# Row transposes between the first adaLN chunks, modulation by feature block, and convolution and adaLN halves between the steps of attention

## The chip, the cores and the metric

The kernel runs on one core of a Trainium2 chip. The metric is the time of one execution on the device in microseconds (us), the median of several runs; smaller is better. An engine is named as the profile names it: PE is TensorE, DVE is VectorE, ACT is ScalarE, POOL is GpSimd, and SP is the engine that issues most of the loads.

## The reference, cut to what matters

Two transformer blocks follow each other over 512 tokens of width 1024. The change touches only the mixer of the first one:

```python
mod   = silu(c) @ w_ada + b_ada              # six rows of 1024: shift, scale, gate, twice
mod_c = silu(c_ctx) @ w_ada + b_ada
hc = modulate(rmsnorm(ctx, g_mix), csh1, csc1)        # 256 context tokens
k_c, v_c = split(hc @ w_in[:, 512:768])
h = modulate(rmsnorm(x, g_mix), sh1, sc1)             # h * (1 + scale) + shift
q, k, v, bg, cg, hv = split(h @ w_in)
att  = windowed_attention(rope(q), rope(k), v, k_c, v_c, sink)
u    = cg * hv
conv = bg * (cw[0] * prev(u) + cw[1] * u + cw[2] * next(u))
x = x + gt1 * (concat([att, conv]) @ w_out)
```

After it come a router with 16 experts of 64 tokens each, then the second block: four feed-forward layers of width 2816, a pooling mixer, a latent attention, and a last norm. All products are made in fp32 from high and low halves, so one product is three matmuls (`mm3`).

## The kernel before

**Weights.** The class `Weights` holds one list of chunks in the order of use. `chunk` plans a load of up to 1 MB, issued on SP into a ring of four buffers (`NR`); `unit` plans a part of a chunk. `next()` hands out the next unit. A unit that is not raw is split first into `whi` (ACT, L161) and `wlo` (DVE, L162), in four buffers, two units ahead. A chunk's buffer comes free when its last unit is split, or, for raw units (the adaLN weights `w_ada`), when the next unit is asked for.

**Order on the engines.** The code is written in one order, and a scheduler puts each engine's instructions into a fixed queue; an engine executes its queue in order. Tiles are given out in rotation: `psA`, `psB` and `psC` have two buffers each in the accumulator memory (PSUM), `pA` of 1024 columns and `pB` and `pC` of 512. Who asks for a third waits until the first is read out.

**Stages before attention.** `ada_rows(0)` multiplies eight 1 MB chunks of `w_ada` (L478) while the six tiles of 128 token rows arrive (`xrow`), get their norm (L275, L262) and are scaled (L495). From its result come `sc1` and `sh1` (scale and shift). Then, for each of the six tiles, `turned` transposes the rows on PE (L294) into `pB` or `pC`, and `modulated_into` makes from each of the eight feature blocks the high half on ACT (L519) and the low half on DVE (L522, L523); 24 matmuls make keys and values of the tile. After the six tiles, q is made for all four tiles of `x` in the two buffers of `pA`. `rope1` rotates keys and q on DVE (L540 to L542); q is split (L599, L600), transposed on PE (L605) and stored as `qT` (L606). The convolution has four blocks of channels; each has three units (`cg`, `hv`, `bg`) of 24 matmuls of 512 columns, in turns in `pB` and `pC`, and a chain on DVE (L621 to L626) that ends in `conv`, which lies in the first half of the tile `X`. In the queue of PE, all four blocks stand ahead of the first score.

**Attention.** There are eight steps, one for each pair of token tile and key head. `scores` makes four heads, each in a `pA` (L687, L689, masks L692), takes the maximum on DVE (L694), the exponential on ACT (L696) and scales (L703). `values` transposes each of four or five key blocks on PE into `pB` (L712), splits (ACT L255, DVE L256) and multiplies into a `pC`. The adaLN groups 1 and 2 (`ada_group`, 8 MB of weights each) stand whole before steps 2 and 5.

**After attention.** `w_out` is applied with the convolution's half of the rows first (`project_out`); L786 reads the first finished tile. Then come norm, router and top-k, the experts and the second block. They aren't changed.

Of the kernel before, what the change touches and what calls it, by code (L numbers as in the profile page):

```python
# [9 lines left out]
F32 = mybir.dt.float32  # L10
# [85 lines left out]
def f(ap):  # L96
    return ap.bitcast(F32)
# [93 lines left out]
def tile_net(ctx, tc, I, out):  # L191
# [20 lines left out]
    def psB():  # L212
        return psh[0].tile([P, 512], F32, name="pB", tag="pB")
# [124 lines left out]
    plan_ada(0)  # L338
    plan_cols(w_in, K, 512, 256, 8, 4)
    plan_cols(w_in, K, 0, 512, 4, 2)  # L340
    for c2 in range(2):
        cs = [W.chunk([(0, P, rows(w_in, 0, K, b0 + c2 * 256, 256))], (P, K, 256)) for b0 in (1280, 1792, 768)]
        for cc in range(2):
            for c in cs:
                W.unit(c, lambda v, cc=cc: v[:, :, cc * P:(cc + 1) * P])
    plan_ada(1)
    plan_ada(2)
    for k0 in (4, 6, 0, 2):
        if k0 >= 4:
# [106 lines left out]
    st = ExitStack()  # L456
    early = st.enter_context(tc.tile_pool(name="early", reuse_waits=RW, bufs=1))

    def token_rows(src, t):
        r = early.tile([P, D], F32, name="xrow", tag="xrow", bufs=6)  # L460
# [6 lines left out]
    def ada_rows(pool, g):  # L467


        bb = pool.tile([P, 512], F32, name="bb", tag="rp1", bufs=1)  # L470
# [3 lines left out]
        p = psB()  # L474
        for k in range(K):
            w = W.next()
            for j in range(4):
                PE.matmul(p[32 * j:32 * j + 32], cb[:, k].rearrange("p s c -> p (s c)"), w[:, j],  # L478
                          start=k == 0, stop=k == K - 1)
        V.tensor_add(bb, p, bb)  # L480
        return bb

    def spread(dst, rows_, j):

# [9 lines left out]
    for r in rows_in:  # L494
# [18 lines left out]
    def modulated_into(pool, dst, t, sc, sh, pick=None):  # L513

        def put(g, m, pv):
            for a in range(m):
                k = g + a
                c_ = slice(t * P, (t + 1) * P)
                A.activation(dst[0][:, k, c_], pv[:, a], AF.Identity, scale=sc[:, k:k + 1], bias=sh[:, k:k + 1])  # L519
            tmp = pool.tile([P, 4, P], F32, name="mtmp", tag="mtmp", bufs=1)  # L520
            for a in range(m):
                V.tensor_scalar(tmp[:, a], pv[:, a], sc[:, g + a:g + a + 1], sh[:, g + a:g + a + 1], op0=OP.mult, op1=OP.add)  # L522
            V.tensor_sub(dst[1][:, g:g + m, c_], tmp, f(dst[0][:, g:g + m, c_]))  # L523
        return put

    hcT = qT.rearrange("p h s -> p (h s)").rearrange("p (s k n) -> p s k n", s=2, k=K)
    hcT = [hcT[:, 0], hcT[:, 1]]
    hT = pair("hT")

    def rope1(src, nt, n, t, pool):  # L530

# [14 lines left out]
    ws = [W.next(), W.next()]  # L546
    kvs = Xf[:, 0:6 * 256].rearrange("p (b n) -> p b n", n=256)

    def turned(b):
        xs, t, s = (hcT, b, 1) if b < TC else (hT, b - TC, 0)  # L550
        transposed(rows_in[b], K, modulated_into(early, xs, t, sc1[:, s], sh1[:, s]))
        return xs, t

    nxt = turned(0)
    for b in range(6):
        xs, t = nxt
        if b < 5:
            nxt = turned(b + 1)
        o = psA()[:, 0:256]
        for k in range(K):  # L560
            mm3(o, [x[:, k, t * P:(t + 1) * P] for x in xs], [x[:, k % 4] for x in ws[k // 4]], k == 0, k == K - 1)
        A.copy(out=kvs[:, b], in_=o)
    split(Vh, Vl, kvs[:, :, P:256])
    for b0 in (0, 2, 4):
        kr = kvs[:, b0:b0 + 2, 0:P]
        if b0:
            kr = rope1(kr.rearrange("p b (h d) -> p b h d", d=HD), 2, KV, b0 - 2, early)
        kr = kr.rearrange("p b (g d) -> p b g d", d=HD)
        kpk = early.tile([P, 2, 2, KV, 2, HD], F32R, name="kpk", tag="kpk", bufs=1)
        for s in range(2):  # L570
            for b in range(2):
                A.copy(out=kpk[:, 0, b, :, s], in_=kr[:, b])
        for s in range(2):
            for b in range(2):
                V.tensor_sub(kpk[:, 1, b, :, s], kr[:, b], f(kpk[:, 0, b, :, s]))
        for s in range(2):
            p = psBC()
# [8 lines left out]
    a0, a1 = psA(), psA()  # L586
    qp = [a0[:, 0:512], a0[:, 512:1024], a1[:, 0:512], a1[:, 512:1024]]
    for u in range(4):
        w = W.next()
        for kk in range(2):  # L590
            k = u * 2 + kk
            for t in range(T):
                mm3(qp[t], [x[:, k, t * P:(t + 1) * P] for x in hT], [x[:, kk] for x in w], k == 0, k == K - 1)
    qks = []
    for t in range(T):
        qr = rope1(qp[t].rearrange("p (o h d) -> p o h d", o=1, d=HD), 1, H, t, early)
        qr = qr[:, 0].rearrange("p (h d) -> p h d", d=HD)
        qk = early.tile([P, H, 2, HD], F32R, name="qk", tag="qk", bufs=1)
        A.copy(out=qk[:, :, 0], in_=qr)  # L599
        V.tensor_sub(qk[:, :, 1], qr, f(qk[:, :, 0]))  # L600
        for g in range(2):
            p = psA()
            pv = p[:, :512].rearrange("p (h t) -> p h t", h=4)
# [5 lines left out]
    for cblk in range(4):  # L609
        p3 = []  # L610
        for _ in range(3):
            p3.append(psBC())
            w = W.next()
            for k in range(K):
                mm3(p3[-1], [x[:, k] for x in w], [x[:, k] for x in hT], k == 0, k == K - 1)
        cg = early.tile([P, S], F32, name="cg", tag="rp1", bufs=1)
        A.copy(out=cg, in_=p3[0])
        u_ = early.tile([P, S + 2], F32, name="convu", tag="convu", bufs=1)
        V.memset(u_[:, 0:1], 0.0)
        V.memset(u_[:, S + 1:S + 2], 0.0)  # L620
        V.tensor_mul(u_[:, 1:S + 1], p3[1], cg)  # L621
        y = early.tile([P, S], F32, name="convy", tag="rp2", bufs=1)
        V.tensor_scalar(y, u_[:, 0:S], cw[:, cblk, 0:1], None, op0=OP.mult)
        V.scalar_tensor_tensor(y, u_[:, 1:S + 1], cw[:, cblk, 1:2], y, op0=OP.mult, op1=OP.add)
        V.scalar_tensor_tensor(y, u_[:, 2:S + 2], cw[:, cblk, 2:3], y, op0=OP.mult, op1=OP.add)
        V.tensor_mul(conv[:, cblk], p3[2], y)  # L626
# [5 lines left out]
    mixT = pair("mixT")  # L632
    for cblk in range(4):
        split(mixT[0][:, 4 + cblk], mixT[1][:, 4 + cblk], conv[:, cblk])
# [7 lines left out]
    cl = []  # L642

    def ada_group(g):
        m = ada_rows(att, g)
        p = psB()
        for c in range(2):
            for j in range(2):
# [57 lines left out]
    def values(n, g, Pt, lo, hi):  # L706
# [11 lines left out]
        split(mixT[0][r, 0:4, n * P:(n + 1) * P], mixT[1][r, 0:4, n * P:(n + 1) * P], ov)  # L718

    todo = [(n, g) for n in range(T) for g in range(KV)]  # L720
    nxt = scores(*todo[0])
    for z, (n, g) in enumerate(todo):
# [740 lines left out]
```

## Time and profile before

| | us |
|---|---|
| median of 3 runs (2702.54 to 2704.97) | 2703.97 |
| profiled execution | 2703.63 |
| its span, from first to last instruction | 2701.6 |

The profiled execution is 2.0 us longer than its span and 0.3 us below the median. PE is busy for 95% of the span; the remaining idle time of PE lies almost all in the first 400 us. In the lines of the timeline, the words in brackets say how long an engine was idle before an instruction, and what it waited for. A granted clock of 1.00 is 2.4 GHz on PE, and 0.50 is 1.2 GHz.

### The profile page before, as it was taken

Reading aid. Unit: us, or ns where it says so; the run is one execution under the profiler, and the core shown is the slowest. Engines: PE = TensorE matmul, PEld = TensorE weight load, DVE = VectorE, ACT = ScalarE, POOL = GpSimd, SP = SyncE. Lnnn points to the kernel's source line nnn. Section 1 sums busy time; section 2 is a strip of 40 time slices with the busy share of each in tenths; the row PEclk is TensorE's granted clock in tenths of the full one; section 3 lists DMA queues with packets and bytes.
Section 4 is the critical chain, followed back from the end, with each engine's and each line's share of the span. In section 5 each row is a group of like instructions: output and inputs, shape, how many; then the busy total and the mean of one; then the engine's idle time right before and its main releaser. Section 6 shows DMA issues by size and latency. Waiting matters only on the chain.

```text
span 2701.6 us, 29081 instructions
## 1 busy us (share of the span) xinstructions
PE 2568.8 (95%) x12042; PEld 1879.9 (70%) x12042; DVE 1066.7 (39%) x1661; ACT 748.4 (28%) x1288; POOL 88.5 (3%) x142
## 2 busy tenths in 40 slices
PE   5988979999998999999999999999999899999999
PEld 3864744333433888878877878887879777878887
DVE  4646441222223433335533334333334566533332
ACT  4324320000002322223322223322223655322221
POOL 1000020000000000000000000000001100000000
PEclk8989979999999999999999999999999999999999
DMA  8226249999998322323222322323232111122321
GB/s 301 67 86 221 71 164 419 414 418 418 416 417 342 124 94 90 105 86 102 74 94 90 106 86 86 108 80 102 78 101 73 63 57 63 63 94 78 108 83 59
DMA packets 179251, 411.89 MB, mean 152 GB/s; under 512 B 7364, under 2 KB 120544, under 8 KB 151472
## 3 DMA queue, kind: packets, MB, share of 16 engines
q1 hardware_dynamic: 176928, 403.73, 40.7%
q0 software_dynamic: 1184, 2.97, 0.4%
q10 hardware_dynamic: 1008, 3.34, 0.3%
q8 instruction: 94, 1.54, 0.2%
q14 instruction: 37, 0.30, 0.0%
HBM read 407.92 MB, written 2.10 MB: 152 GB/s over the span
## 4 chain that ended last, share of the span: by engine, by line
PE 58%; issue 30%; DVE 4%; ACT 3%; DMA 3%; POOL 1%; ACTq 0%; POOLq 0%; DVEq 0%; SPq 0%
PE pA L905 8%; PE pA L247 7%; PE pA L248 7%; PE pA L249 7%; PE pB L905 4%; PE pC L248 2%; PE pC L247 2%; PE pC L249 2%; PE pB L249 2%; PE pB L247 2%; PE pB L248 2%; DMA wraw<-in_w_ada_dram 1%; PE pC L879 1%; PE pC L952 1%; PE ms L1334 1%
## 5 line engine op out<-in xcount | busy, mean ns | idle before, releaser
L161 ACT CAST whi<-wraw 128x1024 fp32r<-128x1024 f32 (+2 forms) x334 | 336.2, 1011 | 1107.6 <-PE pA L248 686.3
L162 DVE TENSOR_TENSOR wlo<-wraw,whi 128x1024 fp32r<-128x1024 f32 (+2 forms) x334 | 392.4, 1177 | 480.1 <-ACT whi L161 472.7
L248 PE MATMUL pA<-xTl,whi 128*128 128x512 f32 (+1 forms) x1536 | 578.7, 377 | 1.6 <-DVE xTl L256 1.6
L249 PE MATMUL pA<-xTh,wlo 128*128 128x512 f32 (+1 forms) x1536 | 578.5, 377 | 0.0
L247 PE MATMUL pA<-xTh,whi 128*128 128x512 f32 (+1 forms) x1536 | 574.7, 382 | 1.5 <-ACT xTh L255 1.3
L247 PEld LDWEIGHTS pA<-xTh,whi 128*128 128x128 f32 x1536 | 290.4, 189 | 76.8 <-ACT sl L989 21.6
L249 PEld LDWEIGHTS pA<-xTh,wlo 128*128 128x128 f32 x1536 | 290.4, 189 | 56.6
L248 PEld LDWEIGHTS pA<-xTl,whi 128*128 128x128 f32 x1536 | 290.8, 189 | 55.2 <-DVE xTl L256 2.1
L991 DVE TENSOR_TENSOR sl<-pA,sl 128x512 f32<-128x512 f32 x88 | 60.9, 692 | 427.3 <-PE pA L249 427.2
L905 PE MATMUL pA<-wraw,wideh 128*64 128x512 f32 x736 | 202.6, 598 | 1.9 <-DMA wraw<-in_w_up_dram 1.4
L249 PE MATMUL pC<-whi,hl 128*128 128x512 f32 x352 | 138.4, 393 | 0.0
L247 PE MATMUL pC<-whi,hh 128*128 128x512 f32 x352 | 138.4, 393 | 0.0
L248 PE MATMUL pC<-wlo,hh 128*128 128x512 f32 x352 | 138.4, 393 | 0.0
L247 PE MATMUL pB<-whi,hh 128*128 128x512 f32 x352 | 138.3, 393 | 0.0
L248 PE MATMUL pB<-wlo,hh 128*128 128x512 f32 x352 | 138.2, 392 | 0.0
L249 PE MATMUL pB<-whi,hl 128*128 128x512 f32 x352 | 138.0, 392 | 0.0
L905 PEld LDWEIGHTS pA<-wraw,wideh 128*64 128x64 f32 x736 | 58.3, 136 | 93.2 <-issue 88.2
L905 PE MATMUL pB<-wraw,hx 128*64 128x512 f32 x344 | 101.0, 597 | 1.1 <-DMA wraw<-in_w_down_dram 1.1
L247 PEld LDWEIGHTS pB<-whi,hh 128*128 128x128 f32 x352 | 66.1, 188 | 15.5 <-DVE X L1040 0.8
L249 PEld LDWEIGHTS pB<-whi,hl 128*128 128x128 f32 x352 | 66.1, 188 | 15.1
L247 PEld LDWEIGHTS pC<-whi,hh 128*128 128x128 f32 x352 | 66.1, 188 | 15.0
L248 PEld LDWEIGHTS pB<-wlo,hh 128*128 128x128 f32 x352 | 66.1, 188 | 14.8
(489 smaller groups left out, 3370.4 us busy)
## 6 DMA issues: line engine op xcount, KB each, us to landing
wraw<-in_w_gate_dram SPq DMA_DIRECT2D x47, 1024.0 KB, 13.3
wraw<-in_w_up_dram SPq DMA_DIRECT2D x45, 1024.0 KB, 12.2
wraw<-in_w_down_dram SPq DMA_DIRECT2D x43, 1024.0 KB, 9.3
wraw<-in_ffn_w_gate_dram SPq DMA_DIRECT2D x40, 1024.0 KB, 5.2
wraw<-in_ffn_w_up_dram SPq DMA_DIRECT2D x40, 1024.0 KB, 5.3
wraw<-in_ffn_w_down_dram SPq DMA_DIRECT2D x32, 1024.0 KB, 4.9
wraw<-in_w_ada_dram SPq DMA_DIRECT2D x24, 1024.0 KB, 9.4
widel<-in_w_up_dram SPq DMA_DIRECT2D x14, 1024.0 KB, 14.0
```

Source lines behind the costliest of these rows:

```text
L161: self.nc.scalar.copy(out=hi, in_=src)
L162: self.nc.vector.tensor_sub(lo, src, f(hi))
L247: PE.matmul(o, a[0], b[0], start=first, stop=False)
L248: PE.matmul(o, a[0], b[1], start=False, stop=False)
L249: PE.matmul(o, a[1], b[0], start=False, stop=last)
L879: PE.matmul(p, ohr[:, t], h[:, t, c_], start=t + z == 0, stop=t + z == T)
L905: PE.matmul(outs[dh][r], x[:, k, r], ws[e][:, j, dh * 512:(dh + 1) * 512], start=k == 0, stop=k == K - 1)
L952: PE.matmul(p, Se[:, t * P:(t + 1) * P], ys[dh][s], start=s == 0, stop=s == 1)
L991: V.tensor_mul(sl, a[:, 512:1024], sl)
L1334: PE.matmul(p[:, :nn], q[a][:, c_], k[b][:, :nn], start=first, stop=False)
```

## The change

The token rows lie in one tile, `xrows`. They are transposed and written back in place during the first adaLN group (`between`, after each chunk), before scale and shift are known. `modulated` then works on one feature block of all context tiles or of all `x` tiles. Keys and values of all six tiles are accumulated at once, in one `pA`, both `pB` and both `pC`. The weights of the convolution come in 12 chunks of 0.5 MB. `conv_block` is a generator that gives up control after each unit and uses only `pC`. Block 0 is started after q and runs beside the rotations. Blocks 1 to 3 and the adaLN groups, in halves of four chunks with a sum of their own, are taken after the steps of attention, by the list in `steps`. Attention's output is kept in `attn` (the second half of `X`) and split per token tile (`settle`), since `mixT` takes the memory of `hT`, which the convolution now reads longer.

```diff
+    def plan_conv(u0, u1):
+        for u in range(u0, u1):
+            b0 = (1280, 1792, 768)[u % 3] + u // 3 * P
+            c = W.chunk([(0, P, rows(w_in, 0, K, b0, P))], (P, K, P))
+            W.unit(c, lambda v: v)
+
+    plan_conv(0, 6)
     plan_ada(1)
+    plan_conv(6, 12)
     plan_ada(2)
...
+        for k0 in (0, 4):
+            p = psB() if g else psA()[:, 0:512]
+            for k in range(k0, k0 + 4):
+                w = W.next()
+                for j in range(4):
+                    PE.matmul(p[32 * j:32 * j + 32], cb[:, k].rearrange("p s c -> p (s c)"), w[:, j],
+                              start=k == k0, stop=k == k0 + 3)
+                if between is not None:
+                    between(k)
+            V.tensor_add(bb, p, bb)
+            yield bb
...
+    def turned(b):
+
+        r = rows_in[b]
         V.tensor_scalar(r, r, row_rstd(early, r, D), None, op0=OP.mult)
-    m = ada_rows(early, 0)
+
+        def put(g, m, pv):
+            (A.copy if g else V.tensor_copy)(out=r[:, g * P:(g + m) * P].rearrange("p (a n) -> p a n", n=P), in_=pv)
+
+        transposed(r, K, put)
+
+    *_, m = ada_rows(early, 0, between=lambda k: turned(k) if k < TC + T else None)
...
+    def modulated(xs, s, k):
+
+        x = xrows[:, :TC] if s else xrows[:, TC:]
+        x, sc, sh = x[:, :, k * P:(k + 1) * P], sc1[:, s, k:k + 1], sh1[:, s, k:k + 1]
+        hi, lo = (v[:, k].rearrange("p (b n) -> p b n", n=P) for v in xs)
+        A.activation(hi, x, AF.Identity, scale=sc, bias=sh)
+        V.tensor_scalar(x, x, sc, sh, op0=OP.mult, op1=OP.add)
+        V.tensor_sub(lo, x, f(hi))
...
+    a0 = psA()
+    kvp = [a0[:, 0:256], a0[:, 512:768], psB()[:, 0:256], psB()[:, 0:256], psC()[:, 0:256], psC()[:, 0:256]]
+    for k in range(K):
+        modulated(hcT, 1, k)
+        modulated(hT, 0, k)
+        for b, o in enumerate(kvp):
+            xs, t = (hcT, b) if b < TC else (hT, b - TC)
             mm3(o, [x[:, k, t * P:(t + 1) * P] for x in xs], [x[:, k % 4] for x in ws[k // 4]], k == 0, k == K - 1)
...
+    first = conv_block(early, 0)
+    next(first)
     split(Vh, Vl, kvs[:, :, P:256])
...
     for t in range(T):
+        if t % 2 == 0:
+            next(first)
         qr = rope1(qp[t].rearrange("p (o h d) -> p o h d", o=1, d=HD), 1, H, t, early)
...
+    def steps():
...
+        ada1, ada2 = ada_group(1), ada_group(2)
+        c1, c2, c3 = (conv_block(att, c) for c in (1, 2, 3))
+        some(c1, 3)
+        yield
+        some(ada1, 1)
+        yield
+        some(ada1, 1)
+        some(c2, 1)
+        yield
+        some(c2, 2)
+        yield
+        some(c3, 2)
+        yield
+        some(c3, 2)
+        some(ada2, 1)
+        yield
+        some(ada2, 1)
+        yield
...
     for z, (n, g) in enumerate(todo):
         cur = nxt
-        if z in (1, 4):
-            ada_group(1 if z == 1 else 2)
         if z + 1 < len(todo):
             nxt = scores(*todo[z + 1])
         values(n, g, *cur)
+        next(beside, None)
+        if z == 6:
+            mixT = pair("mixT")
+            for cblk in range(4):
+                split(mixT[0][:, 4 + cblk], mixT[1][:, 4 + cblk], conv[:, cblk])
+            for b in range(T - 1):
+                settle(b)
+    settle(T - 1)
```

Three places show how the queues change. The first is the queue of DVE at the rotation of q's first tile (`rp` is the rotated tile, `pA` holds q, `wlo` the low half of a weight unit, `qk` q split). Before:

```order
L540 TENSOR_TENSOR rp_821<-pA,cst 128x8x32
L541 TENSOR_TENSOR rp_822<-pA,cst 128x8x32
L540 TENSOR_TENSOR rp_821<-pA,cst 128x8x32
L541 TENSOR_TENSOR rp_822<-pA,cst 128x8x32
L542 TENSOR_TENSOR rp_821<-rp_821,rp_822 128x512
L162 TENSOR_TENSOR wlo<-wraw,whi 128x1024
L600 TENSOR_TENSOR qk<-rp_821,qk 128x8x64
```

Now, at the same place:

```order
L552 TENSOR_TENSOR rp_833<-pA,cst 128x8x32
L553 TENSOR_TENSOR rp_834<-pA,cst 128x8x32
L626 CAST kTl<-pB 128x2x256
L552 TENSOR_TENSOR rp_833<-pA,cst 128x8x32
L553 TENSOR_TENSOR rp_834<-pA,cst 128x8x32
L596 TENSOR_TENSOR convu<-pC,cg 128x512
L554 TENSOR_TENSOR rp_833<-rp_833,rp_834 128x512
L598 TENSOR_SCALAR convy<-convu,cw 128x512
L162 TENSOR_TENSOR wlo<-wraw,whi 128x1024
L599 SCALAR_TENSOR_TENSOR convy<-convu,cw,convy 128x512
L636 TENSOR_TENSOR qk<-rp_833,qk 128x8x64
L600 SCALAR_TENSOR_TENSOR convy<-convu,cw,convy 128x512
```

The product `convu`, which needs the second unit of convolution block 0 from PE, now stands between the products of the rotation and their sum.

The second place is the queue of PE where the first scores stand (`pA<-kTh,qT`). Before, the last matmuls of convolution block 3 stand ahead of them, and nothing between the first heads:

```order
L248 MATMUL pC<-hTl,whi 128x512
L249 MATMUL pC<-hTh,wlo 128x512
L687 MATMUL pA<-kTh,qT 128x256
L687 MATMUL pA<-kTl,qT 128x256
L689 MATMUL pA<-kTh,qT 128x256
L689 MATMUL pA<-kTl,qT 128x256
```

Now the last matmuls of block 0 stand ahead, and 24 of the 32 transposes of q (L640) between the first heads:

```order
L248 MATMUL pC<-hTl,whi 128x512
L249 MATMUL pC<-hTh,wlo 128x512
L704 MATMUL pA<-kTh,qT 128x256
L704 MATMUL pA<-kTl,qT 128x256
L706 MATMUL pA<-kTh,qT 128x256
L706 MATMUL pA<-kTl,qT 128x256
L709 LDWEIGHTS identb
L709 MATMUL pA<-nextb,identb 128x128
L640 MATMUL pB<-cst,qk 128x128 x16
```

The 216 matmuls of the blocks 1 to 3 have moved behind: 72 of them after the eighth head, 58 of these in a row, and 144 from the second half of adaLN group 1 to the first half of group 2.

The third place is an adaLN group in the queue of PE. Before, at the end of group 2:

```order
L689 MATMUL pA<-kTl,qT 128x256
L692 LDWEIGHTS identb
L692 MATMUL pA<-prevb,identb 128x128
L478 MATMUL pB<-wraw,cb 32x512 x12
L649 MATMUL pB<-cst,bb 128x128 x4
L486 MATMUL pB<-bb,cst 128x512 x2
```

Now, at the end of group 1's second half:

```order
L484 MATMUL pB<-wraw,cb 32x512 x4
L248 MATMUL pC<-PTl,Vh 128x512
L249 MATMUL pC<-PTh,Vl 128x512
L484 MATMUL pB<-wraw,cb 32x512 x11
L704 MATMUL pA<-kTh,qT 128x256
L704 MATMUL pA<-kTl,qT 128x256
L706 MATMUL pA<-kTh,qT 128x384
L706 MATMUL pA<-kTl,qT 128x384
```

Each half has 16 of these matmuls close together, and a step's scores and values stand between the halves.

## Rows read from the trace of the kernel before

**Rows 1.** The page: span, and 40 equal slices of it, in tenths.

```profile
span 2701.6 us, 29081 instructions
...
PE   5988979999998999999999999999999899999999
...
DMA  8226249999998322323222322323232111122321
```

**Rows 2.** Busy time of each engine in stretches; granted clock, DMA share, GB/s.

```profile
10.00:41.00 31.00, 14.31 (x69) 2.27 (x69) 5.24 (x10) 6.90 (x12) 5.55 (x13) 0.96 1.02 394
45.50:75.20 29.70, 23.27 (x162) 21.40 (x161) 26.93 (x65) 21.87 (x60) 0.00 (x0) 0.88 0.39 127
75.20:101.80 26.60, 26.59 (x134) 22.36 (x135) 15.65 (x36) 8.91 (x17) 2.01 (x4) 1.00 0.16 50
...
122.40:172.84 50.44, 50.44 (x219) 40.65 (x218) 19.07 (x31) 7.95 (x10) 0.00 (x0) 1.00 0.18 65
...
178.70:192.30 13.60, 11.13 (x45) 9.67 (x46) 8.38 (x22) 6.41 (x18) 0.00 (x0) 0.50 0.09 32
...
260.50:267.40 6.90, 6.11 (x20) 2.78 (x12) 3.49 (x6) 3.01 (x4) 0.00 (x0) 0.51 1.06 293
...
291.00:332.10 41.10, 40.80 (x187) 32.87 (x188) 13.33 (x23) 9.49 (x17) 0.00 (x0) 1.00 0.15 52
...
410.00:600.00 190.00, 186.93 (x803) 76.25 (x799) 42.27 (x81) 13.36 (x23) 0.00 (x0) 1.00 1.01 417
```

**Rows 3.** Groups by line, 0 to 420 us: count, then busy us and mean ns.

```profile
L162 DVE TENSOR_TENSOR wlo<-wraw,whi 128x1024 fp32r<-128x1024 f32 x26 | 31.5, 1222 | 33.6 <-ACT whi L161 33.5
...
L522 DVE TENSOR_SCALAR mtmp<-pB,sc,sh 128x128 f32<-128x128 f32 x24 | 8.3, 404 | 0.7 <-DVE qT L523 0.5
...
L523 DVE TENSOR_TENSOR hTl<-mtmp,hTh 128x512 fp32r<-128x512 f32 x8 | 5.5, 688 | 0.1
...
L495 DVE TENSOR_SCALAR xrow<-xrow,rstd 128x1024 f32<-128x1024 f32 x6 | 4.5, 753 | 14.6 <-POOL rstd L263 14.4
```

**Rows 4.** Timeline of DVE at the rotation of q: start us, us, instruction.

```profile
100.66 0.42 DVE L540 TENSOR_TENSOR rp<-pA,cst 128x256 f32<-128x256 f32 x1 [1.82 <-PE pA L249]
...
105.03 0.42 DVE L540 TENSOR_TENSOR rp<-pA,cst 128x256 f32<-128x256 f32 x1
...
110.85 0.42 DVE L540 TENSOR_TENSOR rp<-pA,cst 128x256 f32<-128x256 f32 x1
...
115.30 0.42 DVE L540 TENSOR_TENSOR rp<-pA,cst 128x256 f32<-128x256 f32 x1
...
121.80 0.68 DVE L606 CAST qT<-pA 128x512 fp32r<-128x512 f32 x1
```

**Rows 5.** Timeline where attention starts.

```profile
177.42 1.28 ACT L696 ACT_TABLE_LOAD   x1 [2.37 <-DVE sm L695]
178.72 0.69 ACT L696 ACTIVATE Pt<-pA,sm 128x512 f32<-128x512 f32 x1
...
179.55 0.58 PE L687 MATMUL pA<-kTh,qT 128*128 128x256 f32 x1 [5.59 <-ACT Pt L696]
```

**Rows 6.** What PE waited for, 178.7 to 332.1 us: total us, times, longest.

```profile
PE pA L687 <- ACT Pt L696: 10.9, 10, 5.6
PE pB L478 <- DMA wraw<-in_w_ada_dram: 5.0, 4, 2.7
PE pB L649 <- DVE bb L480: 2.7, 2, 1.9
PE pC L248 <- DVE PTl L256: 2.5, 6, 0.8
```

**Rows 7.** Loads: issuing queue, count, KB each, median us from issue to landing.

```profile
wraw<-in_ffn_w_gate_dram SPq DMA_DIRECT2D x8, 512.0 KB, 3.8
...
X<-in_x_dram POOLq DMA_DIRECT2D x4, 512.0 KB, 8.4
```

More of the change, by code (lines that the diff above doesn't have):

```diff
@@ L340, in tile_net @@
     plan_cols(w_in, K, 0, 512, 4, 2)
[L341 to L345, printed above, removed]
+    def plan_conv(u0, u1):
[4 more added lines that the diff above has]
+    plan_conv(0, 6)
     plan_ada(1)
+    plan_conv(6, 12)
     plan_ada(2)
@@ L457, in tile_net @@
     early = st.enter_context(tc.tile_pool(name="early", reuse_waits=RW, bufs=1))
+    xrows = early.tile([P, TC + T, D], F32, name="xrows")
     def token_rows(src, t):
-        r = early.tile([P, D], F32, name="xrow", tag="xrow", bufs=6)
+        r = xrows[:, t if src is ctx_in else TC + t]
         nc.scalar.dma_start(out=r, in_=src[t * P:(t + 1) * P])
@@ L465, in tile_net, with ada_rows @@
     b_ada = I["b_ada"]
-    def ada_rows(pool, g):
-        bb = pool.tile([P, 512], F32, name="bb", tag="rp1", bufs=1)
+    def ada_rows(pool, g, between=None):
+        bb = pool.tile([P, 512], F32, name="bb", tag="bb" if g else "cg", bufs=1)
         for j in range(4):
@@ L473, in ada_rows @@
             nc.gpsimd.dma_start(out=bb[32 * j:32 * j + 32], in_=b_ada[:, c0:c0 + 512].to_broadcast([32, 512]))
[L474 to L481, printed above, removed]
+        for k0 in (0, 4):
[9 more added lines that the diff above has]
+            yield bb
     def spread(dst, rows_, j):
@@ L547, in tile_net @@
     kvs = Xf[:, 0:6 * 256].rearrange("p (b n) -> p b n", n=256)
[L549 to L560, printed above, removed]
-            mm3(o, [x[:, k, t * P:(t + 1) * P] for x in xs], [x[:, k % 4] for x in ws[k // 4]], k == 0, k == K - 1)
-        A.copy(out=kvs[:, b], in_=o)
+    a0 = psA()
@@ new lines, in tile_net @@
+    kvp = [a0[:, 0:256], a0[:, 512:768], psB()[:, 0:256], psB()[:, 0:256], psC()[:, 0:256], psC()[:, 0:256]]
[4 more added lines that the diff above has]
+            xs, t = (hcT, b) if b < TC else (hT, b - TC)
+            mm3(o, [x[:, k, t * P:(t + 1) * P] for x in xs], [x[:, k % 4] for x in ws[k // 4]], k == 0, k == K - 1)
+    for b, o in enumerate(kvp):
+        (V.tensor_copy if b % 2 else A.copy)(out=kvs[:, b], in_=o)
@@ new lines, in tile_net, with conv_block @@
+    a0, a1 = psA(), psA()
+    qp = [a0[:, 0:512], a0[:, 512:1024], a1[:, 0:512], a1[:, 512:1024]]
+    for u in range(4):
+        w = W.next()
+        for kk in range(2):
+            k = u * 2 + kk
+            for t in range(T):
+                mm3(qp[t], [x[:, k, t * P:(t + 1) * P] for x in hT], [x[:, kk] for x in w], k == 0, k == K - 1)
+    def conv_block(pool, cblk):
+        for i in range(3):
+            w = W.next()
+            p = psC()
+            for k in range(K):
+                mm3(p, [x[:, k] for x in w], [x[:, k] for x in hT], k == 0, k == K - 1)
+            if i == 0:
+                cg = pool.tile([P, S], F32, name="cg", tag="cg", bufs=1)
+                A.copy(out=cg, in_=p)
+            elif i == 1:
+                u_ = pool.tile([P, S + 2], F32, name="convu", tag="convu", bufs=1)
+                V.memset(u_[:, 0:1], 0.0)
+                V.memset(u_[:, S + 1:S + 2], 0.0)
+                V.tensor_mul(u_[:, 1:S + 1], p, cg)
+                y = pool.tile([P, S], F32, name="convy", tag="cg", bufs=1)
+                V.tensor_scalar(y, u_[:, 0:S], cw[:, cblk, 0:1], None, op0=OP.mult)
+                V.scalar_tensor_tensor(y, u_[:, 1:S + 1], cw[:, cblk, 1:2], y, op0=OP.mult, op1=OP.add)
+                V.scalar_tensor_tensor(y, u_[:, 2:S + 2], cw[:, cblk, 2:3], y, op0=OP.mult, op1=OP.add)
+            else:
+                V.tensor_mul(conv[:, cblk], p, y)
+            yield
@@ L576, in tile_net @@
         for s in range(2):
-            p = psBC()
+            p = psB()
             for b in range(2):
@@ L606, in tile_net @@
             (A.copy if g else V.tensor_copy)(out=qT[:, g * 4:g * 4 + 4, t * P:(t + 1) * P], in_=pv)
[L609 to L626, printed above, removed]
     st.close()
@@ L631, in tile_net @@
     att = st.enter_context(tc.tile_pool(name="att", reuse_waits=RW, bufs=2))
-    mixT = pair("mixT")
-    for cblk in range(4):
-        split(mixT[0][:, 4 + cblk], mixT[1][:, 4 + cblk], conv[:, cblk])
+    attn = Xf[:, 4 * S:8 * S].rearrange("p (c s) -> p c s", s=S)
     gf = att.tile([4, 256], F32, name="gf", bufs=1)
@@ L644, in ada_group @@
     def ada_group(g):
-        m = ada_rows(att, g)
+        halves = ada_rows(att, g)
+        next(halves)
+        yield
+        m = next(halves)
         p = psB()
@@ L717, in values, with some, settle @@
         ov = o[r].rearrange("p (i t) -> p i t", i=4)
-        split(mixT[0][r, 0:4, n * P:(n + 1) * P], mixT[1][r, 0:4, n * P:(n + 1) * P], ov)
+        A.copy(out=attn[r, :, n * P:(n + 1) * P], in_=ov)
+    def steps():
+        def some(g, n):
+            for _ in range(n):
+                next(g, None)
+        ada1, ada2 = ada_group(1), ada_group(2)
[13 more added lines that the diff above has]
+        some(ada2, 1)
+        yield
+        some(ada2, 1)
+        yield
     todo = [(n, g) for n in range(T) for g in range(KV)]
+    beside = steps()
     nxt = scores(*todo[0])
+    mixT = None
+    def settle(n):
+        c_ = slice(n * P, (n + 1) * P)
+        split(mixT[0][:, 0:4, c_], mixT[1][:, 0:4, c_], attn[:, :, c_])
     for z, (n, g) in enumerate(todo):
         cur = nxt
-        if z in (1, 4):
-            ada_group(1 if z == 1 else 2)
         if z + 1 < len(todo):
```

30 lines of the change are left out of this document (4 added, 26 removed).

## The prediction

> **What bounds the kernel now.** I read the page first. In its 40 slices [rows 1] PE is at nine tenths almost everywhere, except in the first six slices, which end at 405 us. From 405 us the loads are at nine tenths or more for about six slices: the stretch of 410 to 600 us has a DMA share of 1.01 at 417 GB/s [rows 2]. So the experts run at the speed of their weights, and what follows at the speed of PE. Neither is changed, and both start when the front ends: a microsecond won or lost before 405 us should arrive whole at the end. I then cut the front into stretches [rows 2]. To 41 us the loads bind (DMA 1.02 at 394 GB/s, PE busy 14.3 of 31 us). In 45.5 to 75.2 us, where keys and values are made, DVE binds (26.93 of 29.7 us), and PE's granted clock is 0.88. From 75.2 to 101.8 and from 122.4 to 172.84 us PE is busy without a gap. That second stretch is nothing but convolution. Then comes attention, where nobody is full: PE waits for the exponentials, for the weights of adaLN and for the split probabilities [rows 6], and twice runs at half its clock (0.50 and 0.51 [rows 2]). The reader is to see that the convolution, dense on PE, stands apart from attention, full of holes; the change lets them meet. But the convolution also covers something now: while DVE rotates q, from 100.66 to 122.5 us [rows 4], PE is never idle.
>
> **Row transposes.** The 48 transposes move into the first adaLN group, with 12 copies. They hide under the loads: PE has 16.7 us idle in 10 to 41 us [rows 2]. By its queue, 16 transposes stand in the middle of the third chunk and may hold that chunk's buffer some 3 us longer. The loads are issued far enough ahead for that, so I take 0; without that cover it would cost up to 3 us.
>
> **Modulation.** Per feature block DVE now does two scalings (512 and 256 elements) and two subtractions, instead of 128-element pieces out of PSUM at 404 ns and subtractions at 688 ns [rows 3]. A scaling of 1024 elements from SBUF takes 753 ns [rows 3]; I estimate 0.5 and 0.35 us for 512 and 256, and 0.69 and 0.42 us for the subtractions: 1.96 us, times 8 is 15.7 us. Four splits of weights at 1.22 us [rows 3] make it 20.6 us, against 26.93 before. PE needs for the 144 key and value matmuls some 16.6 us: 219 matmuls of 512 columns took 50.44 us, 0.230 each [rows 2], and 256 columns cost half. With 8 early q matmuls (1.8 us), and 7.1 us at half clock as before (0.12 times 29.7, doubled), which lose 3.6 us, keys and values end at 45.5 + 16.6 + 1.8 + 3.6 = 67.5 us. The other 88 q matmuls (20.2 us) end at 87.7 us, where they ended at 101.8 us before. That is 14 us earlier.
>
> **The rotation of q loses this again.** In DVE's new queue the product `convu` stands inside the rotation of the first tile. It waits for two units of convolution block 0: 48 matmuls, 11.0 us, and 24 key transposes, 2.2 us (the stretch 75.2 to 101.8 holds 16 of them beside 96 q and 27 half-size matmuls, which leaves 0.09 each). For the key transposes PE waits for ACT, whose next weight split needs a buffer that the convolution's first unit still holds; by the queue some 2.5 us. So DVE goes on at 103.4 us, about where the same rotation stood before (its first product began at 100.66 us and its sum about 1.5 us later). From there it took 20.4 us to the last cast at 122.5 us [rows 4], 4.4 to 5.8 us per tile. Now three weight splits fall out (3.7 us), and the rest of the convolution's chain (four operations on 512 elements, 0.69 us each as [rows 3], 2.7 us) and two score maxima (0.69 us each by the same row, with their short scalars 1.9 us) come in: 21.3 us, to 124.7 us. ACT loads its table only then (1.28 us [rows 5]); the first exponential starts at about 126.4 us, against 178.72 us [rows 5]: **52.3 us earlier**. Meanwhile PE, done with block 0 at some 110 us, has little but 24 transposes and the first heads for 16 us. This is a new hole.
>
> **The convolution is paid behind it.** Blocks 1 to 3 are 216 matmuls at 0.230 us: **49.7 us later**. So the plain move gives 2.6 us. The rest is what they fill.
>
> **What is filled.** Waits for adaLN weights: 5.0 us [rows 6]. Each half now needs four chunks, just the ring, and a step lies between the halves: all 5.0 vanish (worst case none). With the long wait goes the half clock behind it: 6.11 us busy at 0.51 in 260.5 to 267.4 [rows 2], which lost 3.0 us. In group 1 a score head stands between the last matmul and the transposes of the sum: 1.9 of the 2.7 us [rows 6] go. In four of the eight steps convolution matmuls stand between the matmuls of the values, which hides about half of the 2.5 us for split probabilities [rows 6]: 1.3. The waits for exponentials (10.9 us, of which 5.6 is the start itself [rows 6]) stay: the long runs of convolution stand in lumps, not between the heads.
>
> **What is new.** Behind the 5.59 us gap [rows 5] PE ran 13.6 us at half clock, 11.13 of them busy [rows 2]. The new hole is longer. I expect half clock through the eight first heads, which come about as far behind the first exponential as before, plus some 2.7 us, my estimate, since DVE's queue now has other work between their maxima, and a little into block 1: 3.6 us more than before (bounds 0 and 5.6, half of 11.13). The Trainium skill, "TensorE: Matmul & The Clock Gate", section "HAM oscillation — how this bites in real kernels", speaks against the change here: idle gaps take PE back to the half rate, so dense work should be kept together. By that page the loss ends when PE is busy again, by the row it goes on for 13.6 us; with the one the sum below would be some 3.6 us better, with the other 2 us worse. After the lump of 58 matmuls the scores start from empty: 1.5 us. And `w_out` weights are now loaded just before their use, since group 2's second half keeps the ring: 1.5 us (0 to 5).
>
> Hidden: 512-byte pieces of the convolution's chunks (loads of this shape land in 3.8 us [rows 7], a unit keeps PE 5.5 us); the late reload of half of `X` (8.4 us [rows 7], under some 29 us of `w_out` matmuls of the dense stretch 291 to 332.1 us [rows 2]); `settle` and the extra sums (fewer splits on DVE than before, on engines that wait).
>
> **Sum**, on the profiled execution: -52.3 + 49.7 - 5.0 - 3.0 - 1.9 - 1.3 + 3.6 + 1.5 + 1.5 = -7.2; 2703.6 - 7.2 = 2696.4, and 0.3 us more for the median of the runs: 2696.7 us.
>
> **Rivals.**
> *The lumps fill nothing.* The dense runs stand by themselves; DVE and ACT wait meanwhile and scores start again from empty, so the filled 11.2 us come back as other waits. For it: the 58 matmuls in a row. Against: groups of 5 or 6 convolution matmuls stand within the values of blocks 2 and 3. Then -52.3 + 49.7 + 6.6 = +4.0: 2708 us, within 0.2%.
> *The fill pays in full.* The chains run into the lumps, the remaining 5.3 us of exponential waits go, the hole costs no clock: -7.2 - 5.3 - 3.6 - 1.3 and, with the new 3 us gone too, -20: 2684 us. For it: DVE and ACT are both under half busy in 122.4 to 172.84 us. Against: the order of the heads.
> *Slower: the clock stays low while keys and values are made.* Without the row transposes PE gets its work from DVE, 2.07 us per feature block against 1.96 us of DVE. For it: the 0.88 already there [rows 2]. Against: at half clock PE has 4.1 us of work per block, and is full. If all of the 18.4 us there run at half, they take 36.8: 14.8 us more than the 22.0 that I count, and the whole queue behind starts later: +7.6, 2711 us. It turns the sign from 7.2 us on, and reaches 0.2% from 12.6 us on.
>
> **Chances and range.** Forecast 0.5, lumps fill nothing 0.25, full fill 0.13, slower 0.12. This kernel's runs differ by 0.1%, so about 0.2%, 5.4 us, is what can be told from no change. The forecast's own spread (some 6 us, from the hole's 3 us either way, the waits of 5.0 and `w_out`'s 0 to 5) reaches over that line on the slow side in three of ten cases. Faster: 0.35 + 0.13 + a little of the second case, 0.5. Same: 0.15 + 0.2, 0.35. Slower: 0.15. The range must reach the full fill on one side and the first rival with its spread on the other: 2684 to 2709 us.
>
> **What would show it.** q's last matmul near 88 us; the last cast to `qT` at about 125 us and the first exponential near 126; PE mostly idle from about 110 to 138 us, at half clock; no wait of adaLN matmuls for loads behind 140 us; convolution blocks 2 and 3 at full clock without long gaps; the first read of a finished `w_out` tile (L841) near 325 us instead of 332.1. Wrong would make it: the first exponential later than 134 us; waits in the adaLN halves that remain; half clock again between the lumps; or an experts' stage that doesn't start earlier by what the front won.

## The result, and the profile after

The changed kernel takes 2682.36 us (median of 4 runs, 2682.19 to 2682.74), the kernel before beside it 2703.26 us: 20.9 us less, a ratio of 0.9922 with a 95% interval of 0.9905 to 0.994. The prediction said 2696.7 us, 2684 to 2709: the sign was right, the gain was three times what I had reckoned, and it lies below the range. The profiled execution took 2682.74 us.

The page of the changed kernel, to be held against [rows 1]: the span, then 40 slices of it in tenths.

```profile
span 2680.8 us, 29057 instructions
...
PE   6799979999998999998999999999999899999999
...
PEclk9899979999998999999999999999999999999999
DMA  7233469999998322232222222322232111122321
```

PE's second slice falls from 9 to 7: that is the new hole. The third and fourth rise from 8 to 9: attention with convolution in it. The 7 in the sixth, where the experts start, stays. Stretches of the changed kernel, in the columns of [rows 2]:

```profile
10.00:41.00 31.00, 20.44 (x117) 8.99 (x117) 10.62 (x23) 10.21 (x18) 4.46 (x12) 1.00 1.00 368
42.50:64.30 21.80, 21.18 (x146) 20.55 (x147) 19.05 (x37) 13.59 (x22) 0.62 (x1) 0.84 0.49 151
64.30:85.20 20.90, 20.90 (x96) 17.29 (x96) 9.32 (x19) 6.16 (x11) 0.00 (x0) 1.00 0.36 106
...
110.00:124.30 14.30, 6.32 (x27) 5.13 (x25) 7.38 (x17) 5.73 (x10) 2.00 (x4) 0.53 0.05 18
124.30:135.30 11.00, 7.84 (x37) 6.79 (x37) 6.61 (x18) 4.26 (x13) 0.00 (x0) 0.52 0.00 1
135.30:155.80 20.50, 20.50 (x94) 16.63 (x94) 7.60 (x20) 3.69 (x10) 0.00 (x0) 1.00 0.00 1
155.80:192.20 36.40, 33.08 (x199) 18.17 (x198) 22.32 (x47) 15.18 (x34) 0.00 (x0) 0.95 0.40 141
192.20:254.20 62.00, 60.34 (x303) 46.65 (x301) 37.39 (x76) 24.83 (x51) 1.96 (x4) 1.00 0.35 109
...
274.20:313.90 39.70, 39.46 (x175) 31.30 (x176) 13.32 (x16) 12.40 (x16) 1.06 (x2) 1.00 0.67 212
```

The stage of keys and values is now PE's own (21.18 of 21.8 us busy; before, DVE was full there). q's last matmul ends at 85.2 us. The hole is there, 110 to 135 us at half clock, and behind it PE is nearly full. The timeline of the changed kernel, at the first key and value matmul, at the convolution's product in the rotation of q, and at the start of attention (before: [rows 4, 5]):

```profile
42.90 0.80 PE L247 MATMUL pB<-whi,hTh 128*128 128x256 f32 x2 [2.17 <-ACT whi L161]
...
99.51 0.69 DVE L596 TENSOR_TENSOR convu<-pC,cg 128x512 f32<-128x512 f32 x1
...
121.25 1.28 ACT L713 ACT_TABLE_LOAD   x1
122.55 0.69 ACT L713 ACTIVATE Pt<-pA,sm 128x512 f32<-128x512 f32 x1
```

The first exponential comes at 122.55 us, 56.2 us earlier than before. What PE waited for from there to the first read of a finished `w_out` tile, to be held against [rows 6]:

```profile
PE pA L704 <- ACT Pt L713: 5.0, 3, 2.8
PE pC L248 <- DVE PTl L256: 2.7, 3, 2.3
PE pB L729 <- DVE Pt L720: 1.4, 1, 1.4
...
PE pB L666 <- DVE bb L488: 0.8, 1, 0.8
```

No wait for adaLN weights is left, and of the exponentials' 5.0 us 4.5 stand at the start. The first `w_out` read (L841, the old L786) is at 313.91 us instead of 332.06: the front won 18.15 us. The stretch between the two, first in the kernel before, then in the changed one:

```profile
178.72:332.06 153.34, 133.95 (x719) 92.36 (x720) 83.13 (x177) 59.55 (x128) 2.00 (x4) 0.93 0.40 142
122.55:313.91 191.36, 180.70 (x935) 130.46 (x936) 101.08 (x204) 71.59 (x145) 4.14 (x8) 0.96 0.41 139
```

The 216 matmuls more are the convolution. The account closes: 56.17 earlier, 49.7 of convolution later, PE's idle time in this stretch 10.7 instead of 19.4 us, 8.7 less, and 3.0 less for PE's other work, since less of it ran at half clock (11.6 us instead of 17.5). The other 2.7 us lie behind the front (last section).

### The profile page after: what moved, and what is told of

It reads as the page before. It is cut to its first block, busy times and chain, and to the rows that moved or that the text cites. A ratio compares the mean times of both kernels' runs of the same rounds, so it can differ in the third digit from the quotient of the medians.

```text
span 2680.8 us, 29057 instructions
## 1 busy us (share of the span) xinstructions
PE 2561.5 (96%) x12042; PEld 1874.6 (70%) x12042; DVE 1059.8 (40%) x1641; ACT 745.8 (28%) x1263; POOL 87.9 (3%) x142
## 4 chain that ended last, share of the span: by engine, by line
PE 59%; issue 30%; DVE 4%; ACT 3%; DMA 3%; POOL 1%; SPq 0%; ACTq 0%; POOLq 0%; DVEq 0%
PE pA L960 8%; PE pA L247 7%; PE pA L248 7%; PE pA L249 7%; PE pB L960 4%; PE pC L247 3%; PE pC L248 3%; PE pC L249 3%; PE pB L248 2%; PE pB L249 2%; PE pB L247 2%; PE pC L934 1%; PE pC L1007 1%; PE ms L1389 1%; POOL rstd L263 1%
## 5 line engine op out<-in xcount | busy, mean ns | idle before, releaser
L247 PEld LDWEIGHTS pA<-xTh,whi 128*128 128x128 f32 x1536 | 289.8, 189 | 77.0 <-ACT sl L1044 21.8
L960 PEld LDWEIGHTS pA<-wraw,wideh 128*64 128x64 f32 x736 | 58.2, 136 | 93.5 <-issue 87.7
L247 PEld LDWEIGHTS pB<-whi,hh 128*128 128x128 f32 x352 | 66.1, 188 | 15.5 <-DVE X L1095 0.7
L249 PEld LDWEIGHTS pC<-whi,hl 128*128 128x128 f32 x352 | 66.1, 188 | 14.7
## 6 DMA issues: line engine op xcount, KB each, us to landing
wraw<-in_w_gate_dram SPq DMA_DIRECT2D x47, 1024.0 KB, 14.2
wraw<-in_w_up_dram SPq DMA_DIRECT2D x45, 1024.0 KB, 10.7
widel<-in_w_up_dram SPq DMA_DIRECT2D x14, 1024.0 KB, 11.3
```

The costliest lines, as they stand in the source:

```text
L247: PE.matmul(o, a[0], b[0], start=first, stop=False)
L249: PE.matmul(o, a[1], b[0], start=False, stop=last)
L960: PE.matmul(outs[dh][r], x[:, k, r], ws[e][:, j, dh * 512:(dh + 1) * 512], start=k == 0, stop=k == K - 1)
```

## The experiments

Each row gives the first exponential and the first `w_out` read of the profiled execution, then the median and its ratio to the kernel before on the same chip. I read the second column first: it is where the front ends. The same kernel gave 313.9 and 311.6 us there in two profiles, so differences under some 2.5 us in it say nothing.

| kernel | first exp. | `w_out` read | median | ratio (95%) |
|---|---|---|---|---|
| before | 178.7 | 332.1 | 2703.26 | 1 |
| changed | 122.6 | 313.9 | 2682.36 | 0.9922 (0.9905, 0.994) |
| changed, again | 120.9 | 311.6 | 2682.41 | 0.9924 (0.991, 0.9937) |
| front alone | 166.5 | 319.9 | 2690.83 | 0.996 (0.9948, 0.9972) |
| beside attention alone | 132.8 | 324.6 | 2695.42 | 0.997 (0.9961, 0.9979) |
| adaLN groups whole | 120.6 | 314.5 | 2684.6 | 0.9937 (0.9926, 0.9949) |
| one lump | 121.3 | 314.7 | 2684.97 | 0.9934 (0.992, 0.9948) |
| one lump, groups whole | 122.1 | 330.5 | 2699.21 | 0.9984 (0.9973, 0.9994) |
| front and halves alone | 166.4 | 308.6 | 2677.23 | 0.9904 (0.9888, 0.992) |
| halves alone | 177.6 | 318.5 | 2691.68 | 0.9956 (0.9942, 0.997) |
| clock kept up, changed | 122.0 | 313.0 | 2684.27 | 0.993 (0.9917, 0.9942) |
| clock kept up, before | 179.0 | 331.0 | 2700.39 | 0.9993 (0.9984, 1.0002) |
| block 1 in the hole | 127.9 | 298.4 | 2668.21 | 0.9871 (0.9858, 0.9884) |
| and block 2 among the heads | 127.9 | 292.1 | 2662.62 | 0.9853 (0.984, 0.9867) |

**Front alone**, the kernel before with three parts of the diff:

```diff
+    xrows = early.tile([P, TC + T, D], F32, name="xrows")
+    m = ada_rows(early, 0, between=lambda k: turned(k) if k < TC + T else None)
+        modulated(hcT, 1, k)
+        modulated(hT, 0, k)
```

> The kernel before, with the new front alone: the rows are transposed between the chunks of the first adaLN group, modulation goes by feature block, the keys and values of all six row blocks grow together; the convolution (four blocks in a row ahead of attention) and the adaLN groups stay as before. Theory 1, the two parts are independent: in the changed kernel q's last matmul ended at 85.2 us against 101.8, and in the old order the convolution follows on PE without a gap, so those 16.6 us arrive whole: 2703.3 - 16.6 = about 2687 us, first exponential near 162 us; the part beside attention is then worth only 4 to 5 us. Theory 2, the front's gain is lost in the rotation of q unless convolution hides it elsewhere: 2693 to 2700 us. My prediction's own terms (14 us earlier, nothing lost where the convolution covers the rotation) would give 2689 us.

The `w_out` read came 12.2 us earlier, the first exponential as much: what the front wins arrives whole, but it is 12.2 us and not 16.6. Here q's matmuls end at 89.6 us and not 85.2, for the key transposes still stand ahead of them. Theory 1 holds, with its size corrected.

**Beside attention alone**, the changed kernel with the old front:

```diff
-        modulated(hcT, 1, k)
-        modulated(hT, 0, k)
+            nxt = turned(b + 1)
```

> The changed kernel with the old front (row blocks transposed and modulated one after the other behind the first adaLN group), everything beside attention as changed. Theory 1, the parts are independent: the changed kernel's gain without the front's 16.6 us, 4 us below the kernel before: about 2699 us; the hole behind block 0 stands there as in the changed kernel, 16 us later. Theory 2, the part beside attention carries the gain (waits and clock): 2685 to 2691 us. If the hole eats what is filled: 2703 us or more.

7.5 us earlier, between the two theories (the median is 2695.42 us). With the front's 12.2 that makes 19.7, and both together gave 18.2: the two parts add up within the scatter.

**adaLN groups whole**, in the changed kernel:

```diff
-        some(ada1, 1)
-        yield
-        some(ada1, 1)
-        some(c2, 1)
+        some(ada1, 2)
+        yield
+        some(c2, 1)
...
-        some(ada2, 1)
-        yield
-        some(ada2, 1)
+        some(ada2, 2)
```

> The changed kernel with both halves of an adaLN group in one step (group 1 behind the second heads, group 2 behind convolution block 3), so each group again needs eight chunks where the ring holds four. Theory 1, the halves removed the 5.0 us of waits for adaLN weights and some 3 us of half clock behind them: 5 to 8 us slower than the changed kernel, 2687 to 2690 us, with matmuls of adaLN waiting for loads. Theory 2, it is the convolution between that gives the loads their time, and the halves matter little: within 1.5 us of the changed kernel's 2682.4.

Theory 1 falls. Whole groups wait again for weights, but half as long as before, and the `w_out` read moved by 0.6 us (the median by 2.2). PE's waits in that kernel, 120 to 333 us:

```profile
PE pA L704 <- ACT Pt L713: 6.6, 4, 2.8
PE pB L484 <- DMA wraw<-in_w_ada_dram: 2.5, 2, 1.4
```

**One lump**, all three blocks in the first step:

```diff
-    plan_conv(0, 6)
+    plan_conv(0, 12)
     plan_ada(1)
-    plan_conv(6, 12)
...
         some(c1, 3)
+        some(c2, 3)
+        some(c3, 3)
...
```

The loads of blocks 2 and 3 move forward with their matmuls.

> The changed kernel with convolution blocks 1 to 3 in one lump in the first step, adaLN halves in the steps behind; nothing of the convolution between the later heads. Theory 1, what the convolution between heads and values fills (about 8.5 us of waits in the changed kernel's account) comes back: w_out read 6 to 9 us later, near 321 us, total about 2690 us, with waits for adaLN weights, exponentials and split probabilities as in the kernel before. Theory 2, place doesn't matter as long as the convolution stands behind the first heads: within 1.5 us of 313.9 and 2682 us.

Also nothing: 0.8 us (2.6 in the median). By these two runs neither the halves nor the place of the convolution matter. That was a trap, as the next run shows.

**One lump and groups whole**, both edits:

> Both edits of the two earlier runs at once: convolution blocks 1 to 3 in one lump behind the first heads, and adaLN groups whole. Alone they moved the first read of a finished w_out tile from 313.9 to 314.5 (whole groups) and 314.7 us (one lump). Theory 1, convolution between the heads and halves of the groups can replace each other, since either gives the adaLN chunks their time: with neither, the 5.0 us of waits for adaLN weights of the kernel before come back, w_out read near 320 us, total 2688 to 2690 us. Theory 2, neither matters and the gain beside attention comes from the first heads running ahead under the lump: 314 to 316 us, total 2683 to 2686 us.

16.6 us later than the changed kernel. Its waits from 122.1 to 330.5 us, and the whole stretch:

```profile
PE pB L483 <- DMA wraw<-in_w_ada_dram: 6.6, 7, 1.4
PE pA L703 <- ACT Pt L712: 5.7, 7, 2.8
PE pC L248 <- DVE PTl L256: 4.9, 10, 1.0
```

```profile
122.10:330.50 208.40, 188.16 (x935) 133.43 (x936) 99.40 (x203) 70.80 (x145) 4.22 (x8) 0.93 0.39 135
```

The waits for weights are back, and more came with them than theory 1 said: against the changed kernel PE is idle for 9.6 us more (20.2), and busy for 7.5 us more with the same 935 matmuls, at a granted clock of 0.93 instead of 0.96. Halves and convolution between the heads replace each other: one is enough, without both the gain is gone, the front's 12.2 us included. Then the halves should work with no convolution beside attention at all.

**Front and halves alone:**

```diff
-        if z in (1, 4):
-            ada_group(1 if z == 1 else 2)
...
+        if z in (1, 2):
+            next(ada1, None)
+        if z in (4, 5):
+            next(ada2, None)
```

> The new front alone with the adaLN groups in halves (behind the second and third, and behind the fifth and sixth group of heads), no convolution beside attention. The new front alone had its w_out read at 319.9 us with 5.0 us of waits for adaLN weights. Theory 1, halves alone take those waits: w_out read near 315 us, total about 2686 us, so the part beside attention is mostly the halves. Theory 2, without convolution between them the second half waits as long as the group did: 318 to 320 us, total about 2690 us.

They do, and by 11.3 us, more than theory 1 had: this kernel's `w_out` read is at 308.6 us, 5.3 us ahead of the changed kernel, which has the convolution beside attention as well; and its median is 5.2 us lower. Its waits from 166.4 to 308.6 us, and the whole stretch:

```profile
PE pA L695 <- ACT Pt L704: 7.4, 4, 5.6
PE pC L248 <- DVE PTl L256: 4.8, 6, 1.7
PE pC L247 <- ACT PTh L255: 0.8, 3, 0.3
PE pB L720 <- ACT gt L492: 0.7, 1, 0.7
```

```profile
166.40:308.60 142.20, 132.96 (x719) 92.53 (x720) 84.38 (x179) 59.41 (x128) 1.99 (x4) 0.94 0.45 153
```

Against [rows 6] the weights' 5.0, the sum's 2.7 and 3.5 of the exponentials' 10.9 us are gone, only the split probabilities wait 2.3 longer. Of 142.2 us PE is idle for 9.2; in the changed kernel it was 10.7, with 49.7 us of convolution among the heads. So the convolution filled nothing that the halves had left.

**Halves alone**, the same edit on the kernel before:

> The kernel before with the adaLN groups in halves alone (behind the second and third, and the fifth and sixth group of heads); front and convolution as before. With the new front the same edit brought the w_out read from 319.9 to 308.6 us. Theory 1, the halves work in attention alone and don't depend on the front: w_out read near 321 us instead of 332.1, total about 2692 us. Theory 2, they need the new front's earlier loads: 326 us or later, total 2697 us or more.

13.5 us earlier, 1.1 of them already at the first exponential: theory 1. The halves need nothing else of the change. But this edit and the one before it do two things: they cut each group in half, and they take it from ahead of the next heads to behind the values. Whole groups at the new place were not run in these two kernels. In the kernel with one lump both forms stood behind the values, and there the cut alone was worth 15.8 us (314.75 against 330.53).

**Clock kept up**, in the changed kernel (extra matmuls that nobody reads):

```diff
+        for _ in range(n):
+            PE.matmul(idle[0], w, hT[0][:, 0], start=True, stop=True)
...
+        if t > 1:
+            keep_busy(10, qT[:, 7, t * P:(t + 1) * P])
```

> The changed kernel with about 60 extra matmuls of 512 columns whose result nobody reads, put into PE's gaps between 107 and 135 us (10 behind the q transposes of tiles 2 and 3 each, 5 behind each of the first eight score heads); nothing is moved. They are to keep the clock at 2.4 GHz through the hole. Theory 1, the hole's half clock is hidden there (heads and transposes wait for DVE and ACT anyhow): eight heads done and the first read of a finished w_out tile within 1.5 us of the changed kernel's 135.3 and 313.9 us, total 2681 to 2685 us. Theory 2, the half clock is on the path, as my prediction took it for the old gap (half of the busy time): 14.2 us busy at half clock, up to 7 us earlier: w_out read near 308 us, total 2676 us.

Two stretches of that run; in the second the clock is up:

```profile
111.00:124.30 13.30, 11.60 (x46) 9.39 (x47) 5.37 (x13) 4.52 (x8) 2.00 (x4) 0.71 0.07 20
124.30:135.30 11.00, 11.00 (x62) 9.15 (x62) 6.22 (x17) 3.63 (x10) 0.00 (x0) 1.00 0.00 1
```

0.9 us at the `w_out` read: the number of theory 1. But the extra matmuls stand in PE's queue themselves. The third score head in this run, behind a row of them, and the same head in the changed kernel:

```profile
121.83 3.82 PE L635 MATMUL pC<-hTh,qT 128*128 128x512 f32 x16
125.49 0.28 PE L714 MATMUL pA<-kTh,qT 128*128 128x256 f32 x1
```

```profile
123.38 0.58 PE L704 MATMUL pA<-kTh,qT 128*128 128x256 f32 x1 [2.75 <-ACT Pt L713]
```

There it starts 0.83 us after the first exponential, here 3.45 us after it (122.04). Of this delay of 2.6 us 0.9 is left at the eighth exponential, so the heads did go faster at full clock. What full clock without extra work would bring this run does not show.

The same **in the kernel before**, in the gap at the start of attention:

> The kernel before with extra matmuls of 512 columns that nobody reads at the start of attention (20 in the 5.6 us gap ahead of the first exponential, 5 behind each of the first heads). Theory 1, half clock between 178.6 and 192.3 us costs half of the 11.13 us busy there: w_out read 4 to 5.6 us earlier, near 327 us instead of 332.1, total 2698 us. Theory 2, those heads wait for DVE and ACT: within 1.5 us of 332.1 and 2703 us.

```profile
178.60:192.30 13.70, 13.70 (x79) 11.37 (x79) 7.68 (x21) 6.75 (x18) 0.00 (x0) 1.00 0.14 38
```

Full clock where [rows 2] had 0.50, and 1.0 us. Here too PE is full: a head's own five matmuls take 0.70 us instead of 1.36, but five extra ones stand for 1.2 us ahead of the next head. So a clock kept up by extra matmuls gains nothing that can be told from scatter; that half clock costs nothing here neither run shows.

**Block 1 in the hole:**

```diff
+    first, c1 = conv_block(early, 0), conv_block(early, 1)
+    hole = [first, first, c1, c1, c1]
...
-        if t % 2 == 0:
-            next(first)
+        next(hole.pop(0))
```

> The changed kernel with convolution block 1 pulled ahead of attention, its three units among the rotations of q (units at tiles 2 and 3 and behind them), so that the hole on PE from 106 to 135 us is filled; adaLN's first half then comes first beside attention. Theory 1, the hole costs its idle time: the 72 matmuls (16.6 us) leave the lump of 58 and the time behind the first heads, DVE gets three weight splits and a chain more ahead of the first exponential (3 x 1.22 + 4 x 0.69 = 6.4 us): about 10 us faster, 2672 us, first exponential near 129 us, no half clock between 111 and 135. Theory 2, the chain of q's rotation on DVE and ACT slips by what PE wins: 2680 to 2684 us.

15.5 us at the `w_out` read, 14.2 in the median: more than theory 1. The first exponential is 5.4 us later, and PE is busy where it idled. Half clock is not gone, as theory 1 had it, but comes later (0.58 from 127.9 us on):

```profile
106.00:127.90 21.90, 19.66 (x102) 16.05 (x101) 13.79 (x31) 5.37 (x8) 0.00 (x0) 1.00 0.00 0
127.90:140.00 12.10, 8.06 (x39) 7.02 (x39) 6.56 (x18) 5.70 (x17) 0.00 (x0) 0.58 0.01 1
```

**And block 2 among the heads:**

```diff
     nxt = scores(*todo[0])
+    next(beside)
...
```

The list in `steps` and the order of the loads follow.

> The version with convolution block 1 in the hole, and also two units of block 2 (48 matmuls, 11.0 us) among the first heads instead of behind them (one ahead of the second group of heads, one behind it), block 3 one unit per step. Theory 1, the 5.1 us of waits for exponentials at the start and the half clock behind them (8.06 us busy between 127.9 and 140 us) are filled: 5 to 8 us below that version, w_out read near 291 us instead of 298.4, total about 2661 us. Theory 2, the heads come later by what the units take, and the waits only move: 2665 to 2670 us.

6.3 us more at the `w_out` read. The second of those stretches is now full, at full clock:

```profile
127.90:140.00 12.10, 11.53 (x68) 9.23 (x67) 8.24 (x22) 6.45 (x17) 0.00 (x0) 1.00 0.01 1
```

From the first exponential to the `w_out` read, first without block 2 among the heads, then with it:

```profile
127.90:298.40 170.50, 162.62 (x863) 116.03 (x864) 97.72 (x198) 70.88 (x145) 4.16 (x8) 0.97 0.47 156
127.90:292.10 164.20, 156.27 (x854) 111.43 (x853) 95.48 (x195) 69.01 (x142) 4.14 (x8) 1.00 0.45 156
```

The total is theory 1's, the waits are theory 2's: PE is idle for 7.9 us in both, so the waits only moved. What fell is its busy time, by 6.3 us. Nine convolution matmuls now stand ahead of the first exponential (2.1 us); the rest, some 4 us, is work that no longer runs at half clock. Here a clock kept up by work that had to be done anyway was worth something.

With 2662.62 us it is the fastest version, 39 us below the kernel before (2701.97 us beside it) and 20 below the changed one.

## Why the prediction was wrong

**Right.** The row transposes hid under the loads (PE busy for 20.44 of 31 us in 10 to 41 us, 14.31 before). Convolution's 49.7 us came back behind the first exponential. No adaLN matmul waits for weights in the changed kernel. The hole is where I said, at half clock. Of the signs of being wrong one showed, half clock again between the lumps, for 3.3 us (182.7 to 186 us); in the second profile of the same kernel it is not there. `w_out` came 18.15 us earlier and the experts' first matmul 17.9 (371.0 us instead of 388.9), so the front's gain arrived. (The idle time of PE before the change does not lie almost all in the first 400 us, as said at the start: it is 78 of 133 us. The rest is not touched.)

**Term 1, the first exponential, 52.3 earlier: it was 56.2.** Two steps failed. The first is in "Modulation": I let keys and values start at 45.5 us, as before; without the transposes behind the sum they start at 42.90, and q ended at 85.2 instead of 87.7, 2.5 us. The second is in "the rotation of q loses this again": from the end of q to the product `convu` I counted 15.7 us, and it took 14.3 (it stands at 99.51, where I had DVE go on at 103.4). From `convu` to the last cast it took 21.0 us, as reckoned (21.3). The part that is the front's own I put at 14 us; alone it is 12.2.

**Term 2, half clock in the hole, 3.6 us more than before: it was not more.** The step that failed is that the first heads come later behind the first exponential, since DVE has other work between their maxima, and that half clock lasts into block 1. The eighth exponential, before and now:

```profile
193.24 0.69 ACT L696 ACTIVATE Pt<-pA,sm 128x512 f32<-128x512 f32 x1
```

```profile
136.86 0.69 ACT L713 ACTIVATE Pt<-pA,sm 128x512 f32<-128x512 f32 x1 [0.98 <-DVE sm L712]
```

It comes 14.3 us after the first, 14.5 before, and behind the first exponential half clock lasts 12.3 us (to 134.8) with 8.3 us of work in it, where it lasted 13.6 us with 11.13 in [rows 2]. How much of it was lost time, half of the work as I reckoned or less, is not shown: the two runs with extra matmuls do not settle it. The Trainium skill, "TensorE: Matmul & The Clock Gate", section "HAM oscillation — how this bites in real kernels", says that idle gaps take PE to the half rate. The rows agree (0.53 and 0.52 in the hole).

**Terms 3 and 4, restart and late `w_out` weights, +1.5 each: not seen.** Behind the lump (135.30 to 155.80 us) PE waits for 0.5 us in all until 170 us. The stretch 274.2 to 313.9 us is busy for 39.46 of 39.7 us.

**The waits, -5.0, -1.9, -1.3 and -3.0 of clock.** Idle time fell by 8.7 us, where I had 5.2: 8.2 filled, less the 3.0 of new waits that were not seen. The split is not the one I gave. I left the exponentials' other 5.3 us standing; in the changed kernel 0.5 us of waits for exponentials stays behind the start, and the 1.3 for split probabilities did not come (2.7 us, before 2.5). The 3.0 of clock came in size: PE did 5.9 us less of its work at half clock. And the halves alone bring 11.3 us, with the 1.9 for the sum and the clock among them: my 9.9 was near what they bring without the moved convolution. Beside it they bring 0.6.

In the front's sum the miss of 10.95 us (18.15 against 7.2) is thus 3.9 of the first exponential, 3.5 of waits, 3.5 of clock.

**The rivals.** "The lumps fill nothing" was right as a mechanism, given the halves, and wrong as a price: moved beside attention the convolution fills nothing more and costs 5.3 us, the difference between 49.1 us that the attention stretch grew (191.36 against 142.25) and 43.8 us that the first exponential came earlier than in the version with front and halves alone. I had priced that loss at 11.4 us before any filling: the front's 14, less the 2.6 of the plain move. "The fill pays in full" gave 2684 us, near the result, and most of what it named came: the exponentials' waits, no new waits, no more half clock than before. But its cause, chains that run into the lumps, is not what the runs show: the halves alone leave PE idle for 9.2 us, with no convolution beside them. The slower rival did not come: keys and values had clock 0.84, and PE was full.

So, added in this order, of the 18.2 us at the `w_out` read 12.2 come from the front, 11.3 from adaLN in halves (with their new place), and the moved convolution takes 5.3 back, until it is put into the hole that its own move opens.

What stays open: why whole groups and one lump together lose 16.6 us when the waits for weights are 6.6. By PE's time it is 9.6 us of idle time and 7.5 us of slower work, but what of it follows from what wasn't tried.

## What to carry to other kernels

Where two edits might remove the same wait, test them in all four combinations: each taken back alone cost under 1 us at the `w_out` read here, both together 16.6. Before moving dense work beside a stage full of gaps, look at what it covered where it stood, and leave as much of it there as fills that place. A low clock that stood there before the change is no new cost; price only what is more or less of it. Extra matmuls are a poor test of what it costs, for they take the engine's time themselves.

## What the runs showed of the hardware that I had not expected

Half clock stood for 24 us in the changed kernel (110.9 to 134.8 us) and for 13.6 us at the start of attention in the kernel before. Kept up by matmuls that nobody reads, the clock brought 0.9 and 1.0 us, within the scatter; kept up by convolution, in the version with block 1 in the hole, some 4 us. The program behind the `w_out` read, the same in all of these kernels, took 2365.1 us (front alone) to 2371.2 us (groups whole) in fourteen profiled executions, and 2369.5 (before), 2366.9 and 2368.1 us (changed, twice): the 2.7 us that the changed kernel won there are within this scatter, so I don't count them for the change.
